# Splitting the last rows of a rectified row sum between two engines, with fewer steps at the start

## The chip, the cores and the metric

One core of one Trainium2 chip. The time is device microseconds of one execution; medians of several executions are quoted with their number. "Span" is the traced part of an execution, from the first to the last instruction of the kernel that the trace shows; the time of an execution is 1.3 to 1.8 us longer than its span, and that difference turns out to matter here. A transfer "lands" when its semaphore says that its data are there.

## The reference

```python
# x: (32, 512, 1024) float32, 64 MiB
def reference(x):
    return np.sum(np.maximum(x, 0), axis=-1).astype(np.float32)   # (32, 512)
```

## The kernel before

The 16384 rows are dealt out to 128 partitions, 128 rows each: seven transfers of 16 rows per partition (8 MiB) through three buffers, then a tail of 8, 4, 2 and 1 rows, then the last row in three column parts. Rows are rectified and summed in one of two ways: ScalarE rectifies several rows and VectorE sums them (transfers 1 to 6), or one engine does both for one row with an accumulator (`on_act`, `on_dve`), which costs an instruction and a short accumulator read.

```python
STEPS = [4, 5, 7]        # rows per step in a transfer
MIXED = [3, 4, 5]        # the sixth transfer
TAIL = [8, 4, 2, 1]
LAST = [576, 256, 192]   # columns of the last row
...
for c in range(NBIG + 1):
    if c >= NB:
        sp.wait_ge(s_dve, 3 * (c - NB + 1))      # buffer free: VectorE done with transfer c - 3
    ...  # issue transfer c
...
for c in range(NTWO):
    act.wait_ge(s_in[c], 16)
    ...  # two more rows for VectorE alone in the sixth transfer
    for i, n in enumerate(steps):
        ...  # t: the n rows of this step
        act.activation(t, t, AF.Relu).then_inc(s_act, 1)
        dve.wait_ge(s_act, 3 * c + i + 1)
        dve.tensor_reduce(out=res[...], in_=t, axis=X, op=ALU.add).then_inc(s_dve, 1)
...  # the seventh transfer: rows in turn, one to each engine
for r, n, s in tail:                             # the 1-row tail: VectorE alone
    if n > 1:
        act.wait_ge(s, 16)
    dve.wait_ge(s, 16)
    for i in range(r, r + n):
        f = on_act if (i - r) % 2 else on_dve
        f(buf[:, tb, i, :], res[:, j0 + i : j0 + i + 1])

n = LAST[2]
act.wait_ge(s_in[-3], 16)
on_act(parts[0], last[:, n : n + 1]).then_inc(s_tact, 1)
dve.wait_ge(s_in[-2], 16)
on_dve(parts[1], last[:, n + 1 : n + 2]).then_inc(s_tpart, 1)
dve.wait_ge(s_tpart, 1)
dve.wait_ge(s_in[-1], 16)
dve.wait_ge(s_tact, 1)
on_dve(last[:, :], res[:, J - 1 : J]).then_inc(s_tdve, 1)   # third part and the two partial sums
# then SyncE stores the last 16 results of each partition
```

Of the kernel before, what the change touches and what calls it, by code (L numbers as in the profile page):

```python
# [2 lines left out]

P = 128
D = 1024
BIG = 16
NTWO = 6
NB = 3
REGIONS = [112, 16]
CHUNKS = [(0, 0), (0, 16), (0, 32), (0, 48), (0, 64), (0, 80), (0, 96)]  # L10
STEPS = [4, 5, 7]
MIXED = [3, 4, 5]
TAIL = [8, 4, 2, 1]
LAST = [576, 256, 192]


def bass_relu_sum_kernel(
    nc: bass.Bass,
    x: bass.AP,
    out: bass.AP,  # L20
):







    fp32 = mybir.dt.float32
    ALU = mybir.AluOpType  # L30
    AF = mybir.ActivationFunctionType
    X = mybir.AxisListType.X

    B, S, _ = x.shape
    J = B * S // P
    NBIG = len(CHUNKS)
    assert BIG * NBIG + sum(TAIL) + 1 == J == sum(REGIONS) and sum(LAST) == D

    xr = x.rearrange("b s d -> (b s) d")
    of = out.rearrange("b s -> (b s)")  # L40
    start = [sum(REGIONS[:i]) for i in range(len(REGIONS))]
    xv = [
        xr[P * s : P * (s + n), :].rearrange("(p j) d -> p j d", p=P)
        for s, n in zip(start, REGIONS)
    ]
    ov = [of[P * s : P * (s + n)].rearrange("(p j) -> p j", p=P) for s, n in zip(start, REGIONS)]

    buf = nc.alloc_sbuf_tensor("buf", [P, NB, BIG, D], fp32)
    last = nc.alloc_sbuf_tensor("last", [P, LAST[2] + 2], fp32)
    res = nc.alloc_sbuf_tensor("res", [P, J], fp32)  # L50

    n_in = NBIG + len(TAIL) + len(LAST)
    s_in = [nc.alloc_semaphore(f"s_in{i}") for i in range(n_in)]
    s_act = nc.alloc_semaphore("s_act")
    s_dve = nc.alloc_semaphore("s_dve")
    s_fact = nc.alloc_semaphore("s_fact")
    s_fdve = nc.alloc_semaphore("s_fdve")
    s_tact = nc.alloc_semaphore("s_tact")
    s_tpart = nc.alloc_semaphore("s_tpart")
    s_tdve = nc.alloc_semaphore("s_tdve")  # L60
    s_store = nc.alloc_semaphore("s_store")
    s_out = nc.alloc_semaphore("s_out")

    sp, act, dve = nc.sync, nc.scalar, nc.vector


    tb = NBIG % NB


    code = nc.main_func.blocks[0].instructions  # L70
    arrival = next(
        i
        for i, ins in enumerate(code)
        if ins.engine == mybir.EngineType.SP and type(ins).__name__ == "InstDrain"
    )
    for c in range(NBIG + 1):
        if c >= NB:
            sp.wait_ge(s_dve, 3 * (c - NB + 1))
        if c < NBIG:
            g, j = CHUNKS[c]  # L80
            sp.dma_start(out=buf[:, c % NB, :, :], in_=xv[g][:, j : j + BIG, :]).then_inc(
                s_in[c], 16
            )
        if c == 0:
            code.insert(arrival, code.pop())
    r = 0
    tail = []
    for i, n in enumerate(TAIL):
        sp.dma_start(out=buf[:, tb, r : r + n, :], in_=xv[-1][:, r : r + n, :]).then_inc(  # L89
            s_in[NBIG + i], 16  # L90
        )
        tail.append((r, n, s_in[NBIG + i]))
        r += n
    n0, n1 = LAST[0], LAST[0] + LAST[1]
    parts = [buf[:, tb, r, 0:n0], buf[:, tb, r, n0:n1], last[:, 0 : LAST[2]]]
    for k, (lo, hi) in enumerate([(0, n0), (n0, n1), (n1, D)]):
        sp.dma_start(out=parts[k], in_=xv[-1][:, BIG - 1, lo:hi]).then_inc(
            s_in[NBIG + len(TAIL) + k], 16
        )
    sp.wait_ge(s_fact, 1)  # L100
    sp.wait_ge(s_fdve, 1)
    for g in range(len(REGIONS) - 1):
        sp.dma_start(
            out=ov[g][:, :], in_=res[:, start[g] : start[g] + REGIONS[g]]
        ).then_inc(s_store, 16)


    def on_act(t, acc):
        return act.activation(t, t, AF.Relu, accum_out=acc)  # L109

    def on_dve(t, acc):
        return dve.tensor_scalar(  # L112
            out=t, in0=t, scalar1=0.0, scalar2=None, op0=ALU.max, op1=ALU.add, accum_out=acc
        )

    def row(c, i):
        return buf[:, c % NB, i, :], res[:, c * BIG + i : c * BIG + i + 1]

    for c in range(NTWO):
        b, steps = c % NB, STEPS if c < NTWO - 1 else MIXED  # L120
        act.wait_ge(s_in[c], 16)
        if steps is MIXED:
            dve.wait_ge(s_in[c], 16)
            for i in (BIG - 4, BIG - 3):
                on_dve(*row(c, i))
        r = 0
        for i, n in enumerate(steps):
            t = buf[:, b, r : r + n, :]
            act.activation(t, t, AF.Relu).then_inc(s_act, 1)  # L129
            dve.wait_ge(s_act, 3 * c + i + 1)  # L130
            dve.tensor_reduce(  # L131
                out=res[:, c * BIG + r : c * BIG + r + n], in_=t, axis=X, op=ALU.add
            ).then_inc(s_dve, 1)
            r += n
        if steps is MIXED:
            for i in (BIG - 2, BIG - 1):
                on_act(*row(c, i))


    j0 = NBIG * BIG  # L140
    for c in range(NTWO, NBIG):
        act.wait_ge(s_in[c], 16)
        dve.wait_ge(s_in[c], 16)
        for i in range(BIG):
            ins = (on_act if i % 2 else on_dve)(*row(c, i))
            if i >= BIG - 2:
                ins.then_inc(s_fact if i % 2 else s_fdve, 1)
    for r, n, s in tail:
        if n > 1:
            act.wait_ge(s, 16)  # L150
        dve.wait_ge(s, 16)
        for i in range(r, r + n):
            f = on_act if (i - r) % 2 else on_dve
            f(buf[:, tb, i, :], res[:, j0 + i : j0 + i + 1])

    n = LAST[2]
    act.wait_ge(s_in[-3], 16)
    on_act(parts[0], last[:, n : n + 1]).then_inc(s_tact, 1)
    dve.wait_ge(s_in[-2], 16)
    on_dve(parts[1], last[:, n + 1 : n + 2]).then_inc(s_tpart, 1)  # L160
    dve.wait_ge(s_tpart, 1)
    dve.wait_ge(s_in[-1], 16)
    dve.wait_ge(s_tact, 1)  # L163
    on_dve(last[:, :], res[:, J - 1 : J]).then_inc(s_tdve, 1)


    sp.wait_ge(s_tdve, 1)
    sp.dma_start(out=ov[-1][:, :], in_=res[:, start[-1] : J]).then_inc(s_out, 16)
    sp.wait_ge(s_store, 16 * (len(REGIONS) - 1))
    sp.wait_ge(s_out, 16)  # L170


# [1 line left out]
_INS = ['x']  # L174
_OUTS = [((32, 512), 'float32')]


# [21 lines left out]
```

## Time and profile before

| | before |
|---|---|
| time, median of 3 | 161.33 us (161.24 to 161.36) |
| span of the profiled run | 159.9 us |
| profiled instructions | 148 (VectorE 58, ScalarE 55) |
| moved | 67.2 MB |

The lines that carry the argument stand in the prediction below: the chain of waits, the stages between landings, and the tail. In a timeline line the columns are start, duration, engine, source line, operation, output and input, with the idle time before in brackets.

### The profile page before, as it was taken

The numbers are of one execution on the slowest core, as the hardware profiler recorded it, in microseconds if no ns is written. First come the engines' busy times: TensorE is split into PE (matmuls) and PEld (weight loads), VectorE is DVE, ScalarE is ACT, GpSimd is POOL, SyncE is SP. The second block draws the span as 40 slices with busy tenths as digits, with TensorE's granted clock in tenths as the row PEclk, the third lists the DMA queues.
The fourth block names the chain that finished last, engine by engine and source line by source line (L and its number), as shares of the span: only waits on it lengthen the run. The fifth ranks groups of instructions, "written<-read, shape, count | busy, mean of one in ns | idle before, by whom it ended". The sixth has DMA issues, their size and how long they took to land.

```text
span 159.9 us, 148 instructions
## 1 busy us (share of the span) xinstructions
DVE 122.0 (76%) x58; ACT 101.0 (63%) x55; POOL 0.2 (0%) x4
## 2 busy tenths in 40 slices
DVE  0000006989879897998969989699899999598995
ACT  3000059990699808996099941999339980496972
POOL 0000000000000000000000000000000000000000
DMA  7996996996996997989979969969969969899993
GB/s 262 525 525 262 525 525 262 525 525 262 525 492 295 525 459 328 525 377 410 525 312 476 525 262 525 525 262 525 525 262 525 525 262 525 385 402 394 414 407 116
DMA packets 2305, 67.18 MB, mean 420 GB/s; under 512 B 512, under 2 KB 768, under 8 KB 1024
## 3 DMA queue, kind: packets, MB, share of 16 engines
q1 hardware_dynamic: 2304, 67.18, 97.9%
q14 instruction: 1, 0.01, 0.0%
HBM read 67.11 MB, written 0.07 MB: 420 GB/s over the span
## 4 chain that ended last, share of the span: by engine, by line
DMA 69%; ACT 18%; DVE 11%; SPq 1%; issue 0%; DVEq 0%
DMA buf<-in_x_dram 69%; ACT buf L129 18%; DVE res L131 10%; DVE buf L112 1%; SPq L89 1%; DVE last L112 0%; DVEq L163 0%
## 5 line engine op out<-in xcount | busy, mean ns | idle before, releaser
L131 DVE TENSOR_REDUCE res<-buf 128x4 f32<-128x4096 f32 (+3 forms) x18 | 100.4, 5604 | 33.6 <-ACT buf L129 33.6
L129 ACT ACTIVATE buf<-buf 128x4096 f32<-128x4096 f32 (+3 forms) x18 | 80.8, 4553 | 46.3 <-DMA buf<-in_x_dram 46.3
L109 ACT ACTIVATE buf<-buf 128x1024 f32<-128x1024 f32 (+1 forms) x18 | 18.4, 1024 | 9.8 <-DMA buf<-in_x_dram 9.8
L112 DVE TENSOR_SCALAR_CACHE_REDUCE buf<-buf 128x1024 f32<-128x1024 f32 (+1 forms) x19 | 21.3, 1173 | 2.7 <-DMA buf<-in_x_dram 2.5
L109 ACT ACTIVATION_READ_ACCUMULATOR buf<-buf 128x1 f32 x18 | 3.4, 186 | 0.0
L129 ACT ACT_TABLE_LOAD x1 | 1.3, 1283 | 0.8 <-PEq L184 0.8
L112 DVE DVE_READ_ACCUMULATOR buf<-buf 128x1 f32 x19 | 1.6, 83 | 0.0
L112 DVE TENSOR_SCALAR_CACHE_REDUCE last<-last 128x194 f32<-128x194 f32 x1 | 0.4, 356 | 0.1
L184 POOL MEMSET const-bfloat16-1.0<- 128x1 bf16 x1 | 0.1, 102 | 0.0
L184 POOL MEMSET const-uint8-127<- 128x1 uint8 x1 | 0.1, 102 | 0.0
L184 POOL MEMSET const-float32-0.0<- 128x1 f32 x1 | 0.1, 100 | 0.2 <-issue 0.2
L184 POOL MEMSET const-float32-1.0<- 128x1 f32 x1 | 0.1, 99 | 0.0
L112 DVE DVE_READ_ACCUMULATOR last<-last 128x1 f32 x1 | 0.1, 83 | 0.0
## 6 DMA issues: line engine op xcount, KB each, us to landing
buf<-in_x_dram SPq DMA_DIRECT2D x1, 4096.0 KB, 26.7
buf<-in_x_dram SPq DMA_DIRECT2D x1, 2048.0 KB, 31.2
buf<-in_x_dram SPq DMA_DIRECT2D x1, 1024.0 KB, 33.2
buf<-in_x_dram SPq DMA_DIRECT2D x1, 512.0 KB, 34.0
buf<-in_x_dram SPq DMA_DIRECT2D x1, 288.0 KB, 34.3
buf<-in_x_dram SPq DMA_DIRECT2D x1, 128.0 KB, 34.1
buf<-in_x_dram SPq DMA_DIRECT2D x7, 36.3
last<-in_x_dram SPq DMA_DIRECT2D x1, 96.0 KB, 33.9
```

The source lines that it names most:

```text
L89: sp.dma_start(out=buf[:, tb, r : r + n, :], in_=xv[-1][:, r : r + n, :]).then_inc(s_in[NBIG + i], 16)
L109: return act.activation(t, t, AF.Relu, accum_out=acc)
L112: return dve.tensor_scalar(out=t, in0=t, scalar1=0.0, scalar2=None, op0=ALU.max, op1=ALU.add, accum_out=acc)
L129: act.activation(t, t, AF.Relu).then_inc(s_act, 1)
L131: dve.tensor_reduce(out=res[:, c * BIG + r : c * BIG + r + n], in_=t, axis=X, op=ALU.add).then_inc(s_dve, 1)
L184: nc = _bacc.Bacc("TRN2", target_bir_lowering=False, num_devices=1)
```

## The change

The intent: VectorE no longer does the last row but one alone; ScalarE, idle then, takes half of it. The last row's parts are fitted to that, two semaphores of it become one, and the first two transfers take fewer steps.

```diff
-STEPS = [4, 5, 7]
-MIXED = [3, 4, 5]
+ACT_STEPS = [[7, 9], [7, 9], [4, 5, 7], [4, 5, 7], [4, 5, 7], [3, 4, 5]]
+DVE_STEPS = [[7, 9], [7, 4, 5], [4, 5, 7], [4, 5, 7], [4, 5, 7], [3, 4, 5]]
-LAST = [576, 256, 192]
+LAST = [512, 256, 256]
... (the loop over the steps, rewritten for steps that differ between the engines)
-    for r, n, s in tail:
-        if n > 1:
-            act.wait_ge(s, 16)
+    for r, n, s in tail[:-1]:
+        act.wait_ge(s, 16)
...
+    r, _, s = tail[-1]
+    act.wait_ge(s, 16)
+    dve.wait_ge(s, 16)
+    on_act(buf[:, tb, r, 0 : D // 2], half[:, 0:1]).then_inc(s_half, 1)
+    on_dve(buf[:, tb, r, D // 2 : D], half[:, 1:2]).then_inc(s_half, 1)
+    dve.wait_ge(s_half, 2)
+    dve.tensor_tensor(
+        out=res[:, j0 + r : j0 + r + 1], in0=half[:, 0:1], in1=half[:, 1:2], op=ALU.add
+    )
...
-    on_act(parts[0], last[:, n : n + 1]).then_inc(s_tact, 1)
+    on_act(parts[0], last[:, n : n + 1]).then_inc(s_part, 1)
     dve.wait_ge(s_in[-2], 16)
-    on_dve(parts[1], last[:, n + 1 : n + 2]).then_inc(s_tpart, 1)
-    dve.wait_ge(s_tpart, 1)
+    on_dve(parts[1], last[:, n + 1 : n + 2]).then_inc(s_part, 1)
+    dve.wait_ge(s_part, 2)
     dve.wait_ge(s_in[-1], 16)
-    dve.wait_ge(s_tact, 1)
```

## The prediction

> **What bounds the kernel now.** I read the chain of waits first, then a table of stages, then the timeline of the last three microseconds, because the stages decide which part of the change can count at all. The chain of work that ended last, by engine and line:
>
> ```profile
> by line: DMA buf<-in_x_dram 69.2%; ACT buf L129 17.6%; DVE res L131 9.5%; DVE buf L112 1.0%; SPq L89 0.8%; issue 0.3%; DVE last L112 0.2%; DVEq L163 0.0%
> 0.79 40.37 DMA buf<-in_x_dram
> 41.16 0.02 issue
> 41.19 14.05 ACT buf L129 x3
> 55.23 0.02 issue
> 55.26 7.63 DVE res L131
> 62.89 0.02 issue
> 62.90 36.30 DMA buf<-in_x_dram
> ```
>
> Taken alone this says that 27% of the time is ScalarE and VectorE work that frees a buffer. It must be checked against the stages, each from one landing of a transfer to the next (columns: length, busy time of VectorE and ScalarE with their instructions, clock, DMA share, GB/s):
>
> ```profile
> 21.84:41.19 19.35, 15.12 (x3) 14.04 (x4) 0.00 (x0) 1.00 1.00 434
> 41.19:60.54 19.35, 17.47 (x4) 14.04 (x4) 0.00 (x0) 1.00 1.00 434
> 60.54:79.88 19.34, 17.46 (x4) 14.04 (x3) 0.00 (x0) 1.00 1.00 434
> 79.88:99.23 19.35, 17.47 (x4) 14.04 (x4) 0.00 (x0) 1.00 1.00 434
> 99.23:118.57 19.34, 17.46 (x4) 14.04 (x3) 0.00 (x0) 1.00 1.00 434
> ```
>
> The DMA share is 1.00 in every one, at 434 GB/s: an 8 MiB transfer lands each 19.35 us without a gap, although the chain walks over the engines. The reason is in the issues. The timeline of the issuing engine has this for the fourth and fifth transfer:
>
> ```profile
> 43.56 19.67 SPq L81 DMA_DIRECT2D buf<-in_x_dram  x2
> ```
>
> The fourth is issued at 43.56, when its buffer is free, but two others (the second landed at 41.19, the third lands at 60.54) are ahead; the queue would run dry only at about 60.5 less the issue-to-data latency. At about 2.5 us for that (the first transfer landed at 21.84, against 19.35 for its data), the issue has some 60.5 - 2.5 - 43.6 = 14.4 us of slack. The chain's release at 62.90 likewise has 79.9 - 2.5 - 62.9 = 14.5 us. So the kernel is bound by the transfer of 67.1 MB until about 157.3, and after that by a short tail:
>
> ```profile
> 155.04 1.06 ACT L109 ACTIVATE buf<-buf 128x1024 f32<-128x1024 f32 x1 [0.30 <-DMA buf<-in_x_dram]
> 156.32 1.22 DVE L112 TENSOR_SCALAR_CACHE_REDUCE buf<-buf 128x1024 f32<-128x1024 f32 x1
> 157.08 0.68 ACT L109 ACTIVATE buf<-buf 128x576 f32<-128x576 f32 x1 [0.90 <-DMA buf<-in_x_dram]
> 157.47 0.41 DVE L112 TENSOR_SCALAR_CACHE_REDUCE buf<-buf 128x256 f32<-128x256 f32 x1
> 157.67 0.19 ACT L109 ACTIVATION_READ_ACCUMULATOR buf<-buf 128x1 f32 x1
> 158.02 0.36 DVE L112 TENSOR_SCALAR_CACHE_REDUCE last<-last 128x194 f32<-128x194 f32 x1
> 158.41 0.34 SPq L168 DMA_DIRECT2D out_dram<-res  x1
> ```
>
> VectorE takes the last row but one (1024 wide) alone from 156.32, the moment it lands, and is occupied until 157.47, so its 256-wide part of the last row starts about 0.1 us after that landed (issue plus landing time: near 157.38). ScalarE idles 0.90 us meanwhile. Both parts are done near 157.9, the final op starts at 158.02, the store is issued at 158.41, and the span ends 1.5 us later.
>
> **What the Trainium skill says.** "DMA: Bandwidth & Descriptors", section Specifications, gives a fabric ceiling of 435 GB/s; the trace has 434 in the steady stages, so no new order of compute can speed them up. "ScalarE: Activation LUTs", section What ACT_TABLE_LOAD costs, has an ACTIVATE with immediate scale and bias at 186 ns + 0.833 ns an element; the trace agrees (7168 elements predicted 6157 ns, measured 6160). "VectorE: DVE Perf Modes", section The perf-mode tier table, caps a reduce at one element a cycle; the trace agrees (7168 elements in 7620 ns, 4096 in 4418: 1.042 ns an element and 148 ns fixed). The same page's errata section gives (N+151)/0.96 ns for an fp32 tensor_tensor, thus an estimate of 158 ns for N = 1, for which the kernel before has no instance.
>
> **The change, part 1: the first two transfers.** ScalarE now rectifies 7 and 9 rows instead of 4, 5 and 7; it saves one instruction a transfer, some 0.19 us less an overlap of 0.09, in stages where it idles over 5 us. By the slopes above, 9 rows cost ScalarE 0.186 + 9216 x 0.000833 = 7.86 us and VectorE 0.148 + 9216 x 0.001042 = 9.75 us.
>
> First transfer: ScalarE 21.84 to 28.00 to 35.8; VectorE 28.0 to 35.7, then 9 rows 35.9 to 45.7. Before it was done at 43.5, so the fourth transfer is issued 2.1 us later, at 45.7, within 14.4 us of slack. Second transfer: ScalarE 41.19 to 47.3 to 55.1; VectorE 7 rows 47.4 to 55.0, then 4 rows (4.4) and 5 rows (5.5) from 55.2 to 65.0, against 62.9 before; the fifth transfer is issued 2.1 us later, within 14.5 us. Third transfer, split as before: VectorE starts at 65.0 rather than 64.18, works 17.5 us without a wait and ends near 82.6 rather than 82.2. The fourth's first four rows are ready at 83.5 as before, so the delay is gone by then. Worth at the end: 0.00 us.
>
> **Part 2: the last row but one halved.** It lands at 156.30 as before, ahead of anything changed in the last row. Removed from VectorE: an occupancy of 1.15 us (156.32 to 157.47). Added: a 512-wide half. Occupancies until the accumulator read are 1.15 for 1024 and 0.34 for 256 (157.47 to 157.81), so 0.34 + 256 x 0.00105 = 0.61: the read at 156.93, done at 157.01. ScalarE's half: 0.186 + 0.427 = 0.61, less the overlap of 0.09 before its accumulator read of 0.19: 156.32 to about 157.05. The sum of the halves waits for both. Between the end of VectorE's last accumulator read and the final op before lie 0.13 us (157.89 to 158.02, three waits); with one wait I take 0.06 to 0.1, so 157.13, plus 0.16: VectorE is free at about 157.29 instead of 157.47, 0.18 earlier.
>
> **Part 3: the last row as 512, 256, 256.** The three parts carry the same 1024 columns, so the last byte comes as before and its landing stays near 157.7 (issued at 123.78, 33.9 us to landing). The first part lands slightly earlier, by 64 x 128 x 4 bytes at 434 GB/s = 0.08 us: near 157.0 instead of 157.08. ScalarE is busy to 157.05, starts near 157.07 and needs 0.54 + 0.19: done at 157.80 (before 157.86). VectorE's 256 part lands near 157.3; start about 157.35, and 0.42 with the accumulator read: done at 157.77 (before 157.89). So the gate of the final op moves from 157.89 to about 157.80, ScalarE now last, 0.09 earlier; one wait fewer may give 0.03 more. The final op grows from 194 to 258 elements: 64 x 1.042 ns = 0.07 us later. Sum: -0.09 - 0.03 + 0.07 = -0.05 us. Time: 161.33 - 0.05 = 161.28 us.
>
> **Rivals.** (a) The coarse first steps starve the queue. For it: the chain runs over exactly these instructions, and the issuing engine waits on VectorE. Against it: the delay is 2.1 us against over 14 us of slack. Were the slack not real, both late issues could cost up to 2.1 us each and the time would be 163.4 to 165.5. (b) The new sum and its semaphore round trip take the place of the shortened row. For it: 0.26 to 0.29 us of wait and addition between tiny operands, never timed in this trace; if a wait on both engines costs 0.3 rather than 0.1, VectorE is free at 157.5, later than now, and with the wider final op the time is 161.40. (c) VectorE gates fully: if ScalarE's end turns out irrelevant and the three waits before cost 0.05 each, the gain is 0.15 to 0.2 and the time 161.15. (d) The transfer hides it anyhow: the last part landed near 157.7, so even a free VectorE could start the final op no more than some 0.3 us earlier than 158.02; with its growth the floor is about 161.1. All but (a) lie within 0.2% of the time before.
>
> **Range and chances.** The three runs before spread over 0.12 us (161.24 to 161.36). Rivals b to d span 161.1 to 161.4; with a different run's landing times I widen to 161.00 to 161.50. A change of 2% is 3.2 us. The tail holds some 2.2 us from the last row but one to the store, so faster by 2% is impossible without a faster stream: 0.5%. Slower by 2% needs the worst of (a): 0.5%. Within 2%: 99%.
>
> **What would show it.** Stages still at 19.35 us and a DMA share of 1.00; the fourth transfer issued near 45.7, the fifth near 65.1; VectorE at work on the fourth transfer from about 83.5; sixth and seventh landings unchanged at 118.57 and 137.94. In the tail: halves of about 0.63 and 0.68 us from 156.32, an addition of about 0.16 us starting near 157.13, the 256 part near 157.35, the final op of about 0.42 us from 157.90, the store issued near 158.35. I am wrong if the landings shift (a), if the addition starts after 157.3 (b), or if the final op starts before 157.8 or after 158.0.

## More of the kernel before

One more line of the page will be needed, the instructions of each engine:

```profile
DVE 122.0 (76%) x58; ACT 101.0 (63%) x55; POOL 0.2 (0%) x4
```

## The result, and the profile after

| | before | after |
|---|---|---|
| time, median of 6 runs each | 161.32 us (161.20 to 161.36) | 161.17 us (161.00 to 161.21) |
| ratio after to before | | 0.999, 95% interval 0.9977 to 1.0003 |
| span of the profiled run | 159.9 us | 159.8 us |
| VectorE, ScalarE instructions | 58, 55 | 58, 55 |

A ratio is the mean time of one kernel's fast runs over that of the other's of the same rounds, so not quite the ratio of the medians. The interval includes 1, so the runs alone do not prove a gain. The trace has to say what happened.

The stages after, up to the landing of the third transfer and then of the fourth (columns as in the prediction):

```profile
41.19:60.54 19.35, 17.36 (x4) 13.95 (x2) 0.00 (x0) 1.00 1.00 434
60.54:79.88 19.34, 19.34 (x4) 14.04 (x3) 0.00 (x0) 1.00 1.00 434
```

The stages are as long as before, the DMA share is 1.00. In the second one VectorE is busy for all of the 19.34 us: it works off the delay of the coarser steps. The timeline of the issuing engine, SyncE, shows the delay itself:

```profile
45.60 19.75 SPq L84 DMA_DIRECT2D buf<-in_x_dram  x2
```

and that of VectorE where it ends:

```profile
55.18 27.06 DVE L145 TENSOR_REDUCE res<-buf 128x4 f32<-128x4096 f32 x5 [0.15 <-ACT buf L130]
83.54 9.85 DVE L145 TENSOR_REDUCE res<-buf 128x4 f32<-128x4096 f32 x2 [1.30 <-ACT buf L130]
```

The fourth transfer is issued at 45.60 instead of 43.56; VectorE sums without a pause until 82.24, where it ended in the kernel before too (82.23 in its timeline), and starts on the fourth transfer at 83.54 (83.53 before). The delay is gone.

The tail after, to be set against the tail of before in the prediction:

```profile
156.34 0.63 ACT L112 ACTIVATE buf<-buf 128x512 f32<-128x512 f32 x1
156.34 0.69 DVE L115 TENSOR_SCALAR_CACHE_REDUCE buf<-buf 128x512 f32<-128x512 f32 x1
156.88 0.19 ACT L112 ACTIVATION_READ_ACCUMULATOR buf<-buf 128x1 f32 x1
...
157.02 0.63 ACT L112 ACTIVATE buf<-buf 128x512 f32<-128x512 f32 x1
157.09 0.16 DVE L175 TENSOR_TENSOR res<-half 128x1 f32<-128x1 f32 x1
157.40 0.42 DVE L115 TENSOR_SCALAR_CACHE_REDUCE buf<-buf 128x256 f32<-128x256 f32 x1
157.56 0.19 ACT L112 ACTIVATION_READ_ACCUMULATOR buf<-buf 128x1 f32 x1
157.75 0.08 DVE L115 DVE_READ_ACCUMULATOR buf<-buf 128x1 f32 x1
157.88 0.42 DVE L115 TENSOR_SCALAR_CACHE_REDUCE last<-last 128x258 f32<-128x258 f32 x1
...
158.33 0.34 SPq L190 DMA_DIRECT2D out_dram<-res  x1
```

VectorE is free at 157.25 instead of 157.47, but its next work starts at 157.40, only 0.07 earlier. The chain of waits says why; its last lines after are

```profile
123.31 34.07 DMA buf<-in_x_dram
...
157.40 0.44 DVE buf L115 x2
...
157.88 0.43 DVE last L115 x2
```

The chain now enters the tail with a landing, that of the 256-wide part at 123.31 + 34.07 = 157.38, where before it entered with the landing of the row ahead of it. So 0.15 us of the 0.22 that the halving freed are spent waiting for data. From the end of VectorE's part (157.83) to the final op there are 0.05 us instead of 0.13. The final op is 0.07 us longer, and the store is issued at 158.33 instead of 158.41.

Landings shift by up to 0.36 us from one profile to another, for the most part from the first landing on, so below the tail is measured from the start of VectorE's work on the last row but one to the issue of the store: 158.41 - 156.32 = 2.09 us before, 158.33 - 156.34 = 1.99 us after. Over all profiles, the four with the tail of before give 2.06 to 2.09 us, the five with the tail of the change (three of them from the late issues below) 1.94 to 1.99. So the tail is shorter by about 0.1 us in the trace. That the 0.15 us between the medians of the times come from it is likely, but the times alone do not show it.

### The profile page after: what moved, and what is told of

It is laid out like the page before. It is cut to its first block, busy times and chain, and to the rows that moved or that the text cites. A ratio compares the mean times of both kernels' runs of the same rounds, so it can differ in the third digit from the quotient of the medians.

```text
span 159.8 us, 148 instructions
## 1 busy us (share of the span) xinstructions
DVE 121.4 (76%) x58; ACT 101.5 (63%) x55; POOL 0.2 (0%) x4
## 4 chain that ended last, share of the span: by engine, by line
DMA 68%; ACT 18%; DVE 11%; SPq 1%; issue 0%
DMA buf<-in_x_dram 68%; ACT buf L130 18%; DVE res L145 11%; SPq L92 1%; SPq L100 0%; DVE buf L115 0%; DVE last L115 0%
## 5 line engine op out<-in xcount | busy, mean ns | idle before, releaser
L145 DVE TENSOR_REDUCE res<-buf 128x7 f32<-128x7168 f32 (+4 forms) x17 | 100.1, 5923 | 34.0 <-ACT buf L130 34.0
L130 ACT ACTIVATE buf<-buf 128x7168 f32<-128x7168 f32 (+4 forms) x16 | 80.7, 5099 | 46.5 <-DMA buf<-in_x_dram 46.5
L112 ACT ACTIVATE buf<-buf 128x1024 f32<-128x1024 f32 (+1 forms) x19 | 19.0, 1000 | 9.0 <-DMA buf<-in_x_dram 8.9
L115 DVE TENSOR_SCALAR_CACHE_REDUCE buf<-buf 128x1024 f32<-128x1024 f32 (+2 forms) x19 | 20.9, 1146 | 2.8 <-DMA buf<-in_x_dram 2.5
```

The lines of the kernel that those rows point to most:

```text
L112: return act.activation(t, t, AF.Relu, accum_out=acc)
L115: return dve.tensor_scalar(out=t, in0=t, scalar1=0.0, scalar2=None, op0=ALU.max, op1=ALU.add, accum_out=acc)
L145: dve.tensor_reduce(out=res[:, c * BIG + r : c * BIG + r + n], in_=buf[:, c % NB, r : r + n, :], axis=X, op=ALU.add,).then_inc(s_dve, 1)
```

## The experiments

Two theories to begin with. A: only the tail acts, and the coarser steps do nothing. B: the steps contribute. The first four runs undo or isolate parts; they shared one chip and 11 runs of before (161.34, 161.16 to 161.72).

### The tail alone

The changed kernel with the steps of before.

```diff
-ACT_STEPS = [[7, 9], [7, 9], [4, 5, 7], ...]
-DVE_STEPS = [[7, 9], [7, 4, 5], [4, 5, 7], ...]
+ACT_STEPS = [[4, 5, 7]] * 5 + [[3, 4, 5]]
+DVE_STEPS = [[4, 5, 7]] * 5 + [[3, 4, 5]]
```

> The steps of the kernel before (4, 5, 7 rows in each transfer), the whole new tail. Theory A (only the tail acts): same as the changed kernel, some 0.08 us of trace and 0.1 us of time below before, near 161.2; the addition starts at 157.09 and the final op at 157.88 after landings at 156.3. Rival B (the coarser steps contribute through fewer instructions or earlier work): close to before, 161.3.

Measured: 161.45 us (161.14 to 161.48, 5 runs), ratio to before 1.0002 (0.999 to 1.0014). The tail in the trace is as expected, 158.42 - 156.45 = 1.97 us, as in the changed kernel, and the span of the profiled run is 159.9. But the time is not below before. The missing part lies outside the span: time less span is 1.44 to 1.66 us here (median 1.55) and 1.32 to 1.40 in the 11 runs of before. Neither A nor B had that.

### The steps alone

The new steps with the tail, the widths and the waits of before.

```diff
-LAST = [512, 256, 256]
+LAST = [576, 256, 192]
... (tail and last row as in the kernel before)
```

> The coarser steps alone, with the tail of before. Theory A: 161.32 as before, final op at 158.02, stages of 19.35 us, the fourth transfer issued near 45.6 instead of 43.56 with no landing moved. Rival B: 161.2, the gain of the change. Rival a of the prediction (starved queue) would show landings later by up to 2 us.

Measured: 161.74 us (161.65 to 161.95, 6 runs), ratio 1.0028 (1.0016 to 1.0040): slower, clear of noise, which neither theory expected. Again not in the trace: the tail is 158.45 - 156.39 = 2.06 us, the span 159.9. Time less span is 1.75 to 1.80. So this kernel does lose time, outside the span.

### The halving alone

```diff
-LAST = [512, 256, 256]
+LAST = [576, 256, 192]
... (last row with three waits and the steps of the kernel before)
```

> Only the halving of the last row but one; last row 576, 256, 192 with its three waits, steps of before. Theory A: the 256-wide part waits for its landing and starts near 157.40 instead of 157.47; ScalarE's 576-wide part ends at 157.86 as before, so the final op starts at 157.93 to 157.97 instead of 158.02: -0.05 to -0.09 us. Rival (the halving's round trip costs what it saves): final op at 158.02 or later, 161.3 to 161.4.

Measured: 161.56 us (161.47 to 161.62, 5 runs), ratio 1.0013 (1.0001 to 1.0025); time less span 1.57 to 1.68. In the trace the tail is 158.40 - 156.29 = 2.11 us: no gain at all.

```profile
156.29 0.69 DVE L116 TENSOR_SCALAR_CACHE_REDUCE buf<-buf 128x512 f32<-128x512 f32 x1
157.05 0.16 DVE L176 TENSOR_TENSOR res<-half 128x1 f32<-128x1 f32 x1
157.44 0.42 DVE L116 TENSOR_SCALAR_CACHE_REDUCE buf<-buf 128x256 f32<-128x256 f32 x1 [0.23 <-DMA buf<-in_x_dram]
158.00 0.35 DVE L116 TENSOR_SCALAR_CACHE_REDUCE last<-last 128x194 f32<-128x194 f32 x1
```

VectorE is free at 157.21 and then idles 0.23 us for the landing of its part, which follows a 576-wide part: it starts 1.15 us after its work on the row began, exactly as before (157.47 - 156.32). The wait for data has taken the place of the work. The semaphore events in the kept trace of the kernel before show how little there was to free: its 256-wide part landed at 157.42 and VectorE started on it at 157.47. With the first part narrowed to 512, as in the change, the start comes 157.40 - 156.34 = 1.06 us after the work on the row began. The halving alone thus has nothing to gain; halving and widths together with the three waits were not run.

### The widths alone

```diff
-LAST = [576, 256, 192]
+LAST = [512, 256, 256]
```

> Only the widths 512, 256, 256, row not halved, three waits. Theory A: VectorE is held by the whole row until 157.47 as before, the final op starts at 158.02 and is 0.07 us longer: +0.07 us, near 161.4, the store issued near 158.48. Rival (the earlier landing of the first part or ScalarE's earlier end is what counts): at or below 161.3.

Measured: 161.24 us (161.09 to 161.53, 6 runs), ratio 0.9996 (0.9984 to 1.0008). The tail is 158.46 - 156.40 = 2.06 us, not 2.16. The final op is 0.07 longer as expected, but the gap ahead of it shrank:

```profile
157.62 0.19 ACT L109 ACTIVATION_READ_ACCUMULATOR buf<-buf 128x1 f32 x1
157.89 0.08 DVE L112 DVE_READ_ACCUMULATOR buf<-buf 128x1 f32 x1
158.01 0.42 DVE L112 TENSOR_SCALAR_CACHE_REDUCE last<-last 128x258 f32<-128x258 f32 x1
```

VectorE's part ends at 157.97 and the final op starts 0.04 us later, with the same three waits that took 0.13 before. In the chain of waits of the kernel before, that stretch holds a wait of its own on VectorE's queue (DVEq; line 163 is the final op):

```profile
157.90 0.05 DVEq L163
157.95 0.07 issue
```

In the chain of the widths alone there is no such wait. The difference is ScalarE: here it ended at 157.81, long before; in the kernel before it ended at 157.86, 0.03 ahead of VectorE. So the 0.13 was not three waits at a fixed price each; what goes with it is a wait for ScalarE that was satisfied late.

### One wait fewer

The kernel before with one semaphore for both partial sums.

```diff
... (both partial sums count on s_part)
-    dve.wait_ge(s_tpart, 1)
+    dve.wait_ge(s_part, 2)
     dve.wait_ge(s_in[-1], 16)
-    dve.wait_ge(s_tact, 1)
```

> Kernel before with only the two semaphores of the last row merged into one, so VectorE has two waits ahead of the final op instead of three. Theory A: VectorE ends its 256-wide part at 157.89 as before, the gap to the final op falls from 0.13 to about 0.05 us: -0.08 us, final op near 157.94. Rival (the gap is the time of a semaphore from the engine to itself, however many waits): gap 0.13 and no change.

Measured: 161.28 us (161.18 to 161.48, 5 runs), before 161.28 on the same chip; ratio 1.0000 (0.9988 to 1.0013). In the trace, though:

```profile
157.77 0.19 ACT L108 ACTIVATION_READ_ACCUMULATOR buf<-buf 128x1 f32 x1
157.91 0.08 DVE L111 DVE_READ_ACCUMULATOR buf<-buf 128x1 f32 x1
158.03 0.36 DVE L111 TENSOR_SCALAR_CACHE_REDUCE last<-last 128x194 f32<-128x194 f32 x1
```

The gap is 158.03 - 157.99 = 0.04 us and the tail, with the store issued at 158.42, 158.42 - 156.43 = 1.99 us: alone it gains the 0.10 that the whole change gains in the trace. In time it does not show: 0.10 us would be a ratio of 0.9994, inside the interval, so the times neither show it nor rule it out. In all five traces where VectorE has a separate wait for ScalarE and ScalarE ends less than 0.1 us ahead of VectorE, the final op starts 0.15 to 0.16 us after ScalarE's end; with the merged semaphore it starts 0.07 after it here and 0.13 in the changed kernel, where VectorE ends later.

This bears on what the change is worth. On top of the merged semaphore, the halving and the widths let the final op start 0.06 us earlier (1.54 instead of 1.60 us after the work on the row began) and make it 0.07 us longer. The one tail of this run, 1.99 us, is at the edge of the 1.94 to 1.99 of the change: that splitting the row adds anything to the merged semaphore is not shown.

### Three additions instead of one

```diff
-    dve.tensor_tensor(out=res[...], in0=half[:, 0:1], in1=half[:, 1:2], op=ALU.add)
+    dve.tensor_tensor(out=half[:, 2:3], in0=half[:, 0:1], in1=half[:, 1:2], op=ALU.add).then_inc(s_half, 1)
+    dve.wait_ge(s_half, 3)
+    dve.tensor_tensor(out=half[:, 3:4], in0=half[:, 2:3], in1=half[:, 1:2], op=ALU.subtract).then_inc(s_half, 1)
+    dve.wait_ge(s_half, 4)
+    dve.tensor_tensor(out=res[...], in0=half[:, 3:4], in1=half[:, 1:2], op=ALU.add)
```

> The changed kernel with two more dependent one-element operations and waits behind the addition (result the same but for rounding). One addition with its wait takes about 0.08 + 0.16 us, and 0.15 us lie idle before the 256-wide part. Theory A: two more cost 2 x 0.24 = 0.48 us, less the 0.15 idle: +0.33 us against the changed kernel, final op near 158.2. Rival (small operations pipeline or hide behind the landing): below +0.1. Rival b of the prediction (0.3 us each): +0.45 or more.

Measured: 161.78 us (161.70 to 161.86, 5 runs), ratio to before 1.0028. The trace:

```profile
157.10 0.16 DVE L175 TENSOR_TENSOR half<-half 128x1 f32<-128x1 f32 x1
157.30 0.16 DVE L179 TENSOR_TENSOR half<-half 128x1 f32<-128x1 f32 x1
157.49 0.16 DVE L183 TENSOR_TENSOR res<-half 128x1 f32<-128x1 f32 x1
157.57 0.41 DVE L115 TENSOR_SCALAR_CACHE_REDUCE buf<-buf 128x256 f32<-128x256 f32 x1
```

A dependent one-element addition costs 0.20 us from start to start, 0.16 of work and 0.04 of wait, and the independent operation behind it starts 0.08 after it, before it ends. The tail is 158.49 - 156.35 = 2.14 us: 0.40 us of added work cost 0.15 there; the rest was hidden in the wait for the landing and in that overlap. My expected +0.33 was too much for the tail and too little for the time. The span grew more, to 160.3 us, because the final store takes 1.8 us from issue to landing instead of 1.4. This is the only run in which the instruction fetch near the end comes ahead of the store's packets (at 158.9 us; in the other kernels of the table further down it comes after them). Whether that delays the landing was not tested.

### Other widths: 544, 224, 256

```diff
-LAST = [512, 256, 256]
+LAST = [544, 224, 256]
```

> The changed kernel with 544, 224, 256. If VectorE's middle part (157.40 to 157.83) alone gates the final op: it gets 0.03 us shorter, and its landing stays near 157.37: final op near 157.85, -0.03 us. If ScalarE's part or the landing of the last part gates by then: no gain, final op at 157.88 or later. In time both are within the spread of the runs, so the trace decides.

Measured: 161.08 us (160.97 to 161.26, 5 runs), ratio to before 0.9987 (0.9975 to 1.0000); tail 158.14 - 156.20 = 1.94 us, against 1.99 for the change. ScalarE (end 157.63) and VectorE (end 157.61) now finish together. That is more than the expected 0.03 us, but the widths of the change reach 1.94 us as well in one of their five profiles. Part of the lower time is earlier landings (the row started 0.14 earlier than in the changed kernel). The two are not separable by time, and hardly by trace.

### The fourth transfer issued later

Does the issue really have 14 us of slack, as the prediction worked out? The changed kernel, with the issuing engine's wait for the fourth transfer raised to the 3rd, 4th and 5th sum of VectorE (2nd in the change).

```diff
-            sp.wait_ge(s_dve, done[c - NB])
+            sp.wait_ge(s_dve, K if c == NB else done[c - NB])   # K = 3, 4 or 5
```

> The changed kernel, the fourth transfer issued when VectorE has done the first step of the second transfer, at about 55.05 us, 9.4 us later than in the changed kernel. Slack theory: 60.54 - 2.5 - 55.05 = 3.0 us still to spare, no landing moves, 161.2. Rival (a queue with fewer requests waiting runs slower): a stage longer than 19.35 us and more than 161.5.

> The changed kernel, but the fourth transfer is issued only when VectorE has done the first two steps of the second transfer, at about 59.6 us instead of 45.6. By the slack theory (latency of issue to first data 2.5 us) it lands at 59.6 + 21.84 = 81.4 instead of 79.88: +1.6 us, 162.8. With a latency of 2.0 us: +1.1, 162.3. If the queue had no slack at 45.6 at all, it would be +14 us.

> The changed kernel, the fourth transfer issued when VectorE is done with the second, at about 65.05 us. Slack theory: lands at 65.05 + 21.84 = 86.9 instead of 79.88, and everything after shifts by the same: +7.0 us, 168.2; the DMA share of that stage falls. With the latency that the run at 59.6 us shows, the number must follow from it: one microsecond of issue, one of time.

| fourth transfer issued at | its work starts at | time |
|---|---|---|
| 45.60 (the change) | 79.89 | 161.17 (6 runs) |
| 55.11 | 79.96 | 161.22 (4 runs) |
| 59.64 | 81.53 | 162.79 (4 runs) |
| 64.92 | 86.92 | 168.12 (1 run, state unknown) |

The stages of the run issued at 59.64, from the landing of the second transfer on:

```profile
41.19:60.54 19.35, 17.39 (x4) 13.95 (x2) 0.00 (x0) 1.00 0.88 379
60.54:79.88 19.34, 19.34 (x4) 14.04 (x3) 0.00 (x0) 1.00 1.04 434
```

The DMA share falls to 0.88 in the stage in which the queue runs dry. From issue to work there are 81.53 - 59.64 = 21.89 us, of which 19.35 are data: a latency of 2.5 us. Up to 55.11 the issue costs nothing, at 59.64 it costs 1.6 us, and 5.3 us later 5.3 us more. The slack in the change is 60.5 - 2.5 - 45.6 = 12.4 us. All three came as expected, and the queue did not run slower while it was short but not empty (issue at 55.11).

### What lies outside the span: one more VectorE instruction, two more on ScalarE

The first runs left 0.2 to 0.4 us outside the span. What they have in common is a number of instructions that differs from before. The halving adds two to ScalarE (an activation and its accumulator read, 57), the coarser steps take two away (53), the change does both (55, as before). The instruction fetches, on the queue called q14, move as well. The DMA view of the changed kernel between 159 and 160 us has one packet of it (columns: packets, MB, share of 16 engines' time in that stretch), and so has the kernel before:

```profile
q14 instruction: 1, 0.01, 3.3%
```

The steps alone have none there; theirs comes between 161 and 162 us, after the span:

```profile
q14 instruction: 1, 0.01, 3.4%
```

The tail alone has two, one in each of these stretches. Two more runs vary the count and nothing else that matters. The first is the steps alone, with the first sum of VectorE in three steps:

```diff
-DVE_STEPS = [[7, 9], [7, 4, 5], ...]
+DVE_STEPS = [[7, 4, 5], [7, 4, 5], ...]
```

> The coarser steps alone were slow by 0.4 us outside the traced span, with an instruction fetch at 161.2 us instead of 159.6. This run is the same with the first transfer's sum on VectorE in three steps again, so VectorE has its 58 instructions of before and ScalarE still 53. Theory C (the fetch hangs on VectorE's count): the fetch is back at 159.6, time less span 1.36, time 161.3. Rival D (it hangs on ScalarE's 53): still late, time less span 1.8, time 161.7. Rival E (not the count but the steps as such): still 161.7 as well, but then the next run shows nothing.

Measured: 161.59 us (161.50 to 161.70, 5 runs), ratio 1.0020 (1.0007 to 1.0032). The fetch is back inside the span, at 159.7, so its timing goes with VectorE's count in this pair of runs; but time less span is still 1.68 to 1.75. Theory C is right about the fetch and wrong about the time, which stays with ScalarE's 53 as D had it.

```profile
DVE 121.7 (76%) x58; ACT 100.8 (63%) x53; POOL 0.2 (0%) x4
```

The second is the kernel before, with the first transfer rectified in five steps:

```diff
-ACT_STEPS = [[4, 5, 7]] * 5 + [[3, 4, 5]]
+ACT_STEPS = [[4, 5, 3, 2, 2]] + [[4, 5, 7]] * 4 + [[3, 4, 5]]
```

> The kernel before in tail and steps, but ScalarE rectifies the first transfer in 4, 5, 3, 2 and 2 rows, so it has 57 instructions as in the two runs with a halved row, and VectorE 58; the work is the same, and 0.2 us of fixed cost lies in 5 us of idle time. Theory C (ScalarE's count over 55 puts one more instruction fetch behind the end): a second fetch near 161.1, time less span 1.55 to 1.6, time 161.5 to 161.6. Rival (the extra fetch of those runs comes from VectorE's 59 instructions or from the halving): one fetch near 159.6, time less span 1.36, time 161.3.

Measured: 161.43 us (161.26 to 161.58, 5 runs), ratio 1.0008 (0.9994 to 1.0022). The time itself is not clear of noise. Time less span is: 1.41 to 1.60 (median 1.53) against 1.31 to 1.40 in the nine runs of before on that chip. A second fetch appears at 161.4 us.

```profile
DVE 122.0 (76%) x58; ACT 101.2 (63%) x57; POOL 0.2 (0%) x4
```

The kernels by ScalarE's count, without the three late issues (medians of time less span, where spans are given to 0.1 us, so that a single difference is good to 0.05; the profiled run's instruction fetches near the end):

| kernel | ScalarE | VectorE | time less span, us | fetches at, us |
|---|---|---|---|---|
| steps alone | 53 | 57 | 1.78 | 161.2 |
| steps, one more on VectorE | 53 | 58 | 1.70 | 159.7 |
| before | 55 | 58 | 1.36 | 159.6 |
| the change | 55 | 58 | 1.38 | 159.6 |
| widths alone | 55 | 58 | 1.36 | 160.0 |
| one wait fewer | 55 | 58 | 1.38 | 159.6 |
| 544, 224, 256 | 55 | 58 | 1.37 | 159.4 |
| three additions | 55 | 60 | 1.38 | 158.9 |
| two more on ScalarE | 57 | 58 | 1.53 | 159.9 and 161.4 |
| tail alone | 57 | 59 | 1.55 | 159.5 and 161.1 |
| halving alone | 57 | 59 | 1.62 | 159.5 and 161.1 |

The late issues, with 55 and 58, had 1.36, 1.34 and, in the single run, 1.32. So with 55 the difference is the same to 0.06 us whatever VectorE has; with 53 it is 0.34 to 0.42 longer than before, with 57 0.17 to 0.26. For 57 a fetch after the end goes along with it, with identical work in the run that only splits steps; that the fetch itself is what takes the time was not shown. For 53 no fetch explains it, and the cause stays open. The counts are those of the profile, without waits and issues; no run separates the count from other ways in which the instruction streams differ. The widths alone have their only fetch at 160.0, just after the span, at no cost.

So the new steps may have a use: they take off ScalarE the two instructions that the halving puts on. The tail alone was at 1.55, the change is at 1.38.

## Why the prediction was right or wrong

The time, 161.17 us, lies in the range, 0.11 below the 161.28 predicted.

- **What bounds the kernel.** Right, and now tested: the transfers set the time to 157 us, and the chain over the engines is not the limit. Rival a falls: the issue had the slack computed, with the latency of 2.5 us that was read off the first transfer. Rival d did not bind: the last part landed at 157.76 by the semaphore events of the trace, and the final op started at 157.88.
- **Part 1, the steps, "worth 0.00".** Right inside the span: issue at 45.60 (predicted 45.7), VectorE through with the third transfer at 82.24 (82.6: the sum left out that reductions in a row overlap a little, five taking 27.06 us from 55.18), the fourth begun at 83.54. Wrong outside of it: the steps alone cost about 0.4 us, and with the new tail they save about 0.2. The prediction had no term for the time outside the span, as the page of before gives no hint of one. In the total nothing of it is left, with ScalarE at 55 instructions as before; for the prediction that was luck.
- **Part 2, the halving.** The addition started at 157.09 (157.13) and took 0.16; VectorE was free at 157.25 (157.29). The estimate of 158 ns, from the formula in the errata section of "VectorE: DVE Perf Modes", agrees with the 160 ns of the trace. As the addition started before 157.3, rival b falls. The 0.22 us freed are mostly not used, as the next part lands at 157.38; the prediction had that too, with 157.35 as the start (measured 157.40). One reading was off: in the kernel before the 256-wide part did not land about 0.1 us ahead of VectorE's start but 0.05, at 157.42, so the row in front of it held it up less than the prediction took.
- **Part 3, the last row.** The final op is 0.07 us longer, as worked out (0.42). The gate was named wrongly: ScalarE was done at 157.75, not 157.80, as its second activation started at 157.02, before its accumulator read for the first was over (157.07), and VectorE was the last, at 157.83.
- **The mis-sized term** is the wait ahead of the final op: 0.03 us were allowed for one wait fewer; the gap fell by 0.08, from 0.13 to 0.05. It was not the number of waits that was dear: three cost only 0.04 us in the widths alone, where ScalarE ended early, and the merged one cost 0.04 where ScalarE ended late. Why a late separate wait takes longer is not shown. Rival c had said 161.15 with costlier waits. Its number was nearest; its reading, 0.05 us for each of three waits, is contradicted by the widths alone.
- **Sum.** Predicted -0.09 - 0.03 + 0.07 = -0.05 us. Measured from the row to the store in the trace, -0.10: the gate -0.08 (1.49 instead of 1.57 us after the work on the row began), the gap -0.08, the final op +0.07, with 0.01 of rounding.

## What to carry to other kernels

When work is taken off the engine in front of a transfer, look up when the data for the next piece lands: the gain ends there, unless the sizes are moved with it, and the sizes moved can cost as much elsewhere, here in the longer final op. Where a result needs two engines, try one semaphore on which both count: here it brought as much in the trace as the whole change. And when a change of under half a microsecond in a short kernel does not show in the trace, compare time less span and the number of instructions of each engine before taking it for noise.

## What the Trainium skill lacked or had wrong

- "Runtime: NRT & Kernel Launch", section Instruction fetch mechanics, calls the cost of crossing a block of instructions mostly hidden. This case does not decide it: a fetch that moved from 161.2 to 159.7 us changed the time outside the span by only 0.08, but a second fetch behind the end went along with 0.17 to 0.26 more. The section has no word on how the time outside the traced span follows an engine's instruction count: 1.32 to 1.38 us with 55 instructions on ScalarE, 1.70 to 1.78 with 53, 1.53 to 1.62 with 57.
- "DMA: Bandwidth & Descriptors" fits about 2.0 us of fixed cost for transfers issued from GpSimd, and for those from SyncE gives only a first-byte latency of about 0.6 us. Here an 8 MiB load issued from SyncE took 2.5 us more than its data from issue to the first work on it: the first one 21.84 - 19.35, the one issued at 59.64 as the queue ran out 81.53 - 59.64 - 19.35.
- None of the pages used here has the cost of a wait by where it stands: a separate wait for ScalarE that is satisfied last put 0.15 to 0.16 us between ScalarE's end and VectorE's operation; with one merged semaphore it was 0.05 and 0.07 in the two traces where ScalarE was late (544, 224, 256 and one wait fewer).
